# One feature tile at a time in the first stage of a diffusion backbone: token rows loaded first, root chains moved, context tiles moved into the second half

## The chip, the cores and the metric

The kernel runs on one core of a Trainium2 chip. The metric is the device time of one execution in microseconds; lower is better. A core has five engines with a queue each: TensorE (PE in the profile; its weight loads are PEld), VectorE (DVE), ScalarE (ACT), GpSimd (POOL) and SyncE (SP, which here only starts transfers). They run side by side and wait for each other through semaphores. Data lies in SBUF (128 partitions); matmuls write to PSUM banks of 128 x 512 numbers, which ScalarE and VectorE read out.

## The reference, cut to what matters

```python
silu_c, silu_cc = silu(c), silu(c_ctx)
# layer 0, attention; layer 1 (a convolution branch on the latent tokens only) is not touched
shift, scale, gate = split((silu_c @ ada_w[0] + ada_b[0])[:, None, :], 3)
h_lat = rmsnorm(x, norm_g[0]) * (1 + scale) + shift            # x: 1024 tokens x 1024
shift_c, scale_c, _ = split(silu_cc @ ada_w[0] + ada_b[0], 3)
h_ctx = rmsnorm(ctx, norm_g[0]) * (1 + scale_c) + shift_c      # ctx: 256 tokens x 1024
proj = h_lat @ w_in                                            # q (16 heads), k, v (4 heads each), z
kv_c = h_ctx @ w_in[:, q_end:v_end]
o = windowed_attention(rope(q), rope(k), v, kc, vc, sink)      # window 128, all context keys, a sink
x = x + gate * ((o * silu(z)) @ w_out)
```

Everything is float32. A product of two float32 matrices is made of three matmuls in the rounded type fp32r: high part by high part, high by low and low by high, where the low part is what rounding left over.

## The kernel before

**Order of the work.** The kernel is one straight program: a first stage that normalises and modulates the tokens and computes the first heads' projections, then attention over 16 heads with the remaining projections filled in between, the output projection, the convolution branch and its projection. The change touches the first stage alone, and a few lines that reach into the second. The first stage works on features in tiles of 128 (`KT` = 8 of them, index `kt`) and on tokens in halves of 512.

**Who sets the order.** The kernel is scheduled by a framework, which orders each engine's instructions by a model of time, except for the engines that `pin(...)` names: `InOrder` then keeps these in the order of the program. TensorE is always pinned; `pin("PVA")` (line 477) adds VectorE and ScalarE for the beginning of the stage, `pin("PV")` (line 497) leaves ScalarE to the scheduler for the rest of it. Since all engine calls go through `InOrder.call`, every row of the profile has line 89; rows are told apart by their tiles.

**Names in the rows.** `x_page` are token rows (128 tokens x 1024, float32), `araw_page` modulation weights, `arow_half` the row of modulation sums, `mod` the shift and scale columns of a tile, `wraw_page`, `whi_page`, `wlo_page` a projection weight and its high and low part, `hf_page`, `hh_page`, `hl_page` a modulated feature tile (full, high, low), `hch_page`, `hcl_page` the same for context, `junk_page` the squares, whose sums are kept. PSUM tiles are `psg` (two banks), `pso` (`ps_o(0)` and `ps_o(1)`, one bank each) and `pss` (two tiles of two banks). `zerr_page` are zeros on which `spin(n)` runs n matmuls that compute nothing used.

**The stage, step by step.**
- Loads (lines 317 to 334) are started on SP: `ada_load(pr)` fetches the shift and scale weights of a pair of feature tiles (8 transfers of 256 KB in runs of 1 KB, and the biases), `load_rows` token rows (512 KB each), `wsA.load` a projection weight (512 KB in runs of 512 bytes). The first pair's modulation weights stand ahead of the first half's token rows.
- `sums` squares rows on ScalarE, `rstd_of` makes 1/sqrt of the mean by a root on ScalarE and six small operations on VectorE, `scale_rows` multiplies the rows by it.
- `ada_mm(pr)` multiplies silu(c) by the modulation weights of a pair (8 matmuls of 512 columns in four column groups), VectorE adds the biases, `ada_cols(pr)` turns the row into columns with a small matmul each, VectorE writes them to `mod`.
- `turn` transposes four token blocks of a feature tile, `x_tile` modulates the result: ScalarE writes the high part, VectorE the full tile, VectorE or GpSimd the low part. ScalarE and VectorE read the same PSUM bank one after the other.
- `x_mm(kt, half, acc, which)` multiplies feature tile `kt` with the weights of k, q and v (9 matmuls of 512 columns).
- The loop over pairs `pr` (line 500) does this for the first half of the tokens, with everything for pair `pr + 1` issued ahead. At `pr == 2` the roots of the second half's rows (`normalise(xs1, ...)`) stand on VectorE behind the add of pair 3 and ahead of its modulation columns. The context's tiles (`c_tile`) are made in the last two pairs.
- Then `finished0` takes k, q and v out of PSUM (the rotary step `rope` copies halves of a head between partitions by DMA), `ctx0("k", 0)` projects the context's keys, and the second loop does `x_mm` for the other 512 tokens, with `ctx0("v", 2)` at `kt == 3`. It ends with `scores(0, 0)`, the first scores of attention.

## Time and profile before

| | us |
|---|---|
| median of three runs | 1727.83 (1724.6, 1727.83, 1729.25) |
| the profiled execution | 1728.0 |
| its span | 1726.2 |
| TensorE's granted clock over the span | 0.993 |
| VectorE, ScalarE, GpSimd busy | 1090.0, 873.8, 899.1 |
| moved by DMA | 242.44 MB |

How to read it: the page gives one execution. Busy time of a matmul is from its issue to its modelled end, so a matmul of 512 columns has some 0.39 us though the next one starts 0.23 after it. Rows in order of time have the start, the duration of the whole group, the engine, the operation with written <- read tiles, the shape, the count, and in brackets how long the engine stood idle and for whom. Rows of stretches give the busy time of each engine with the number of instructions, then TensorE's granted clock, the share of time in which the DMA engines were busy, and GB/s.

### The profile page before, as it was taken

What the parts mean: (1) busy time and instruction counts of PE and PEld (TensorE: products, weight loads), DVE (VectorE), ACT (ScalarE), POOL (GpSimd) and SP (SyncE); (2) the same over time, 40 slices, a digit from 0 to 9 for tenths busy, and PEclk for the clock granted to TensorE, in tenths of its full rate; (3) what the DMA queues carried; (4) which work ended last, traced back from release to release, by engine and by line L of the source; (5) the groups of instructions that cost most, each with busy time, mean ns of one, the idle gap of its engine ahead of it and who ended that gap; (6) DMA issues with size and microseconds to landing.
All of it is one profiled execution on the core that took longest, in us unless ns stands there. A gap on an engine that the chain in (4) does not pass through costs nothing.

```text
span 1726.2 us, 23896 instructions
## 1 busy us (share of the span) xinstructions
PE 1692.5 (98%) x8420; PEld 1423.5 (82%) x8420; DVE 1090.0 (63%) x2077; ACT 873.8 (51%) x1532; POOL 899.1 (52%) x745
## 2 busy tenths in 40 slices
PE   8899999999999999999999999999999999999997
PEld 5688888888888888888888888888888888787886
DVE  4555553555355453555315179999999999867823
ACT  4555544555355444545334355565665564466731
POOL 1255654666546564643101257999898888130400
PEclk9999999999999999999999999999999999999999
DMA  9233442444334443436776733011121302377971
GB/s 335 85 110 123 155 140 76 136 151 148 96 124 141 156 129 93 141 115 210 261 252 247 247 94 107 21 50 37 43 80 37 92 31 80 122 260 244 330 269 49
DMA packets 195323, 242.44 MB, mean 140 GB/s; under 512 B 11798, under 2 KB 126790, under 8 KB 195204
## 3 DMA queue, kind: packets, MB, share of 16 engines
q1 hardware_dynamic: 188516, 230.10, 40.1%
q10 hardware_dynamic: 6688, 10.83, 2.5%
q8 instruction: 66, 1.08, 0.3%
q14 instruction: 53, 0.43, 0.1%
HBM read 188.70 MB, written 41.69 MB: 133 GB/s over the span
## 4 chain that ended last, share of the span: by engine, by line
PE 91%; DMA 3%; ACT 2%; DVE 2%; POOL 1%; issue 1%; SPq 0%; ACTq 0%; DVEq 0%; POOLq 0%
PE psg L89 47%; PE pss L89 24%; PE pso L89 20%; DMA low_page<-in_conv_w_out_dram 1%; DMA rope_half<-rope_half 1%; POOL rope_half L89 0%; DMA wo_page<-in_conv_w_out_dram 0%; DMA x_page<-in_x_dram 0%; DMA araw_page<-in_ada_w_dram 0%; SPq L89 0%; ACT junk_page L89 0%; ACT hh_page L89 0%; ACT lhi_half L89 0%; ACT x_page L89 0%; POOL wlo_page L89 0%
## 5 line engine op out<-in xcount | busy, mean ns | idle before, releaser
L89 POOL TENSOR_TENSOR odd_half<-odd_half,prod_half 128x513 f32<-128x513 f32 (+2 forms) x252 | 314.2, 1255 | 23.0 <-ACT prod_half L89 9.6
L89 PE MATMUL psg<-hh_page,whi_page 128*128 128x512 f32 x600 | 236.2, 394 | 0.0
L89 PE MATMUL psg<-hl_page,whi_page 128*128 128x512 f32 x600 | 235.1, 392 | 0.0
L89 PE MATMUL psg<-hh_page,wlo_page 128*128 128x512 f32 x600 | 234.6, 391 | 0.0
L89 ACT ACTIVATE prod_half<-ubuf,dww 128x513 f32<-128x513 f32 (+2 forms) x252 | 165.7, 675 | 115.9 <-POOL odd_half L89 112.1
L89 POOL TENSOR_TENSOR wlo_page<-wraw_page,whi_page 128x512 fp32r<-128x512 f32 (+1 forms) x106 | 177.5, 1691 | 88.2 <-ACT whi_page L89 60.3
L89 POOL TENSOR_SCALAR p_page<-p_page,sc 128x640 f32<-128x640 f32 (+1 forms) x128 | 99.6, 778 | 225.6 <-DVE sc L89 218.4
L89 PE MATMUL psg<-h2h_page,whi_page 128*128 128x512 f32 x464 | 181.9, 392 | 0.0
L89 PE MATMUL psg<-h2h_page,wlo_page 128*128 128x512 f32 x464 | 180.6, 389 | 0.0
L89 PE MATMUL psg<-h2l_page,whi_page 128*128 128x512 f32 x464 | 180.6, 389 | 0.0
L89 DVE SCALAR_TENSOR_TENSOR pss<-ubuf,dww,pss 128x512 f32<-128x512 f32 (+3 forms) x270 | 172.6, 672 | 0.1
L89 DVE SCALAR_TENSOR_TENSOR pss<-ubuf,wsum,pss 128x512 f32<-128x512 f32 (+3 forms) x270 | 172.0, 672 | 0.2
L89 DVE TENSOR_TENSOR ptlo<-pss,pthi 128x640 fp32r<-128x640 f32 (+1 forms) x144 | 103.5, 719 | 86.3 <-ACT pthi L89 85.1
L89 ACT ACTIVATE p_page<-p_page,sc 128x641 f32<-128x641 f32 (+1 forms) x128 | 102.6, 802 | 76.9 <-DVE sc L89 72.6
L89 ACT ACTIVATE pthi<-pss 128x640 fp32r<-128x640 f32 (+1 forms) x144 | 88.8, 617 | 103.7 <-PE pss L89 97.3
L89 PEld LDWEIGHTS psg<-hh_page,wlo_page 128*128 128x128 f32 x600 | 113.1, 188 | 24.7
L89 PEld LDWEIGHTS psg<-hh_page,whi_page 128*128 128x128 f32 x600 | 113.1, 188 | 19.5
L89 PEld LDWEIGHTS psg<-hl_page,whi_page 128*128 128x128 f32 x600 | 113.2, 189 | 18.7
L89 ACT ACTIVATE whi_page<-wraw_page 128x1024 fp32r<-128x1024 f32 x88 | 92.5, 1052 | 58.5 <-PE psg L89 20.9
L89 PE MATMUL pso<-h2h_page,whi_page 128*128 128x512 f32 x304 | 118.3, 389 | 0.0
L89 PE MATMUL pso<-h2l_page,whi_page 128*128 128x512 f32 x304 | 118.3, 389 | 0.0
L89 PE MATMUL pso<-h2h_page,wlo_page 128*128 128x512 f32 x304 | 118.3, 389 | 0.0
(239 smaller groups left out, 4008.6 us busy)
## 6 DMA issues: line engine op xcount, KB each, us to landing
wraw_page<-in_conv_w_in_dram SPq DMA_DIRECT2D x48, 512.0 KB
wraw_page<-in_attn_w_in_dram SPq DMA_DIRECT2D x40, 512.0 KB
wol_page<-wolA SPq DMA_DIRECT2D x32, 512.0 KB
wo_page<-in_attn_w_out_dram SPq DMA_DIRECT2D x32, 512.0 KB
wo_page<-in_conv_w_out_dram SPq DMA_DIRECT2D x32, 512.0 KB
wol_page<-wolC SPq DMA_DIRECT2D x32, 512.0 KB
rope_half<-rope_half ACTq DMA_DIRECT2D x80, 128.0 KB
araw_page<-in_ada_w_dram SPq DMA_DIRECT2D x32, 256.0 KB
```

Source lines behind the costliest of these rows:

```text
L89: r = f(*a, **k)
```

## The change

- **Single feature tiles.** `ada_load`, `ada_mm`, `ada_cols` and `mods` work on one feature tile instead of a pair: 4 transfers of 256 KB, now in runs of 512 bytes; 8 matmuls of 256 columns; an add of 256 columns; two column matmuls. The loop runs over `kt`, with the modulation of `kt + 1` issued around the matmuls of `kt`. All the low parts of the first half's tiles are made by VectorE (before, every second one by GpSimd).
- **Loads.** Token rows go first, then the modulation weights of tile 0, then projection weights and further tiles; then the small vectors (biases and such, before in the middle of the loop), the second half's rows and the context's. The mask and the sinks are loaded by SP instead of ScalarE's queue.
- **Scaling of rows.** The first half's four rows are scaled by VectorE, GpSimd, ScalarE, GpSimd (before V, V, A, A), ahead of `ada_mm(0)`; the spins are redistributed.
- **Roots.** The squares of the second half's rows are issued at `kt == 4`, their roots and scaling at the end of `kt == 6`, behind the tile work of feature 7 on VectorE and ahead of the second half's first tile.
- **Context.** Its rows are squared at `kt == 6`, scaled at the second half's `kt == 0`, its tiles made at `kt` 2 to 5 of the second half's loop, two in each, and `ctx0("k")` and `ctx0("v")` follow at 6 and 7.
- **Second half.** `finished0` takes v out first; the rotary steps start one tile later; the pages of q and v are allocated at `kt == 5`, and the weight of the next projection is loaded there (before at 0) and split at 6 (before at 5).

```diff
-    def ada_load(pr):
-        R[pr] = hp.alloc(F32, None, "arow")
-        G.memset(R[pr][:, 0:512], 0.0)
-        araw[pr] = [pg.alloc(F32, [2, 2, 256], "araw") for _ in range(4)]
-        for i in range(4):
+    def ada_load(kt):
+        if kt % 2 == 0:
+            R[kt // 2] = r = hp.alloc(F32, None, "arow")
+            G.memset(r[:, 0:512], 0.0)
             for j in range(2):
...
+        araw[kt] = [pg.alloc(F32, [4, 2, P], "araw") for _ in range(2)]
+        for i in range(2):
+            for j in range(2):
+                SY.dma_start(out=araw[kt][i][:, :, j],
+                             in_=ada_w[0, i * 512:i * 512 + 512, j * D + kt * P:j * D + kt * P + P]
                              .rearrange("(k p) n -> p k n", p=P))
...
     spin(4)
+    xs0 = load_rows(x[0, 0:512], 4)
     ada_load(0)
-    xs0 = load_rows(x[0, 0:512], 4)
     wsA.load()
     ada_load(1)
     wsA.load()
     wsA.load()
     ada_load(2)
+    ada_load(3)
+    ada_load(4)
+    ada_load(5)
...
-    ada_load(3)
+    ada_load(6)
+    ada_load(7)
+    vec_pg = load_vecs()
+    xs1 = load_rows(x[0, 512:1024], 4)
     cx = load_rows(ctx[0], 2)
...
+    def ada_mm(kt):
+        o = ps_o(0)[:, 0:256]
+        for i in range(2):
+            rv = araw[kt][i].rearrange("p a b c -> p a (b c)")
+            for k in range(4):
+                PE.matmul(o[32 * k:32 * k + 32], c32[:, 4 * i + k, :], rv[:, k], start=i == 0, stop=i == 1,
+                          tile_position=(0, 32 * k))
...
+        r = R[kt // 2][:, kt % 2 * 256:kt % 2 * 256 + 256]
         tt(V, r, o, r, ALU.add)
...
     pin("PVA")
-    ada_split(0)
-    spin(10)
+    spin(28)
     ss0 = sums(xs0, (A, A, A, A))
+    r0 = rstd_of(ss0, D, 4)
+    scale_rows(xs0, r0, (V, G, A, G))
     ada_mm(0)
     ada_cols(0)
-    spin(18)
-    r0 = rstd_of(ss0, D, 4)
-    wsA.split(lambda: scale_rows(xs0, r0, (V, V, A, A)))
-    xs1 = load_rows(x[0, 512:1024], 4)
     tps = [turn(xs0, kt, ps_g) for kt in range(2)]
-    for kt in range(2):
-        x_tile(tps[kt], kt, 0, V)
-    spin(5)
-    pg.free(zer_r)
-    x_mm(0, 0, acc0, (0,))
-    x_mm(1, 0, acc0, (0,))
+    x_tile(tps[0], 0, 0, V)
+    wsA.split()
+    spin(4)
+    ada_mm(1)
+    x_mm(0, 0, acc0, (0,))
+    ada_cols(1)
+    x_tile(tps[1], 1, 0, V)
     pin("PV")
-    ada_split(1)
+    spin(6)
+    pg.free(zer_r)
     wsA.split()
     wsA.split()
-    for pr in range(NPR):
...
-        if pr == 2:
-            normalise(xs1, ss1, (G, G, A, G))
...
+    ctodo = deque(range(KT))
+    for kt in range(1, KT):
+        nx = kt + 1
+        if nx < KT:
+            ada_mm(nx)
+        x_mm(kt, 0, acc0, (0,))
+        if kt == 1:
+            x_mm(0, 0, acc0, (1,))
+        if nx < KT:
+            tp = turn(xs0, nx, ps_g)
+            ada_cols(nx)
+            x_tile(tp, nx, 0, V)
+        else:
+            turn_vecs()
+            x_tile(turn(xs1, 0, ps_g), 0, 1, V)
+        x_mm(kt, 0, acc0, (1,))
+        if kt == 1:
+            x_mm(0, 0, acc0, (2,))
+        x_mm(kt, 0, acc0, (2,))
+        if kt == 4:
             ss1 = sums(xs1, (A, A, A, A))
-        if pr == 2:
+        if kt == 6:
             pg.free(*xs0)
             cos, sin = (pg.alloc(F32, [1024], n) for n in ("cos", "sin"))
...
+            normalise(xs1, ss1, (G, V, A, V))
+            ssc = sums(cx, (A, A))
+    x_tile(turn(xs1, 1, ps_g), 1, 1, V)
...
-    A.dma_start(out=mask[:, 0:640], in_=k_mask)
-    A.dma_start(out=sink, in_=attn_sink.partition_broadcast(P).rearrange("p o h -> p (o h)"))
+    SY.dma_start(out=mask[:, 0:640], in_=k_mask)
+    SY.dma_start(out=sink, in_=attn_sink.partition_broadcast(P).rearrange("p o h -> p (o h)"))
...
-    finished0(0, acc0, ropes=ropes0)
-    ctx0("k", 0)
+    finished0(0, acc0, (2, 0, 1), ropes0)
...
     for kt in range(KT):
         x_mm(kt, 1, acc1, range(3))
         if kt + 2 < KT:
             x_tile(turn(xs1, kt + 2, lambda: ps_o(kt % 2)), kt + 2, 1, G if kt % 2 and kt > 1 else V)
-        if kt > 2 and ropes0:
+        if kt == 0:
+            normalise(cx, ssc, (V, A))
+        if kt > 3 and ropes0:
             ropes0.popleft()()
-        if kt == 3:
-            ctx0("v", 2)
-        if kt >= 2 and tails:
+        if 1 < kt < 6:
+            c_tile(ctodo.popleft(), ps_s)
+            c_tile(ctodo.popleft(), lambda: ps_o((kt + 1) % 2))
+        if kt == 5:
+            for i in (1, 2):
+                d0[i].extend(target("kqv"[i], 0))
+            pg.free(*xs1)
+            wsA.load()
+        if kt >= 6 and tails:
             tails.pop(0)()
-        if kt == 0:
-            wsA.load()
-        if kt == 5:
-            pg.free(*xs1)
+        if kt == 6:
             wsA.split()
+            ctx0("k", 0)
+        if kt == 7:
+            ctx0("v", 2, lambda: ps_o(1))
         if kt == KT - 1:
             scores(0, 0)
```

137 lines of the change are left out of this document (44 added, 93 removed).

## The prediction

> **What bounds the kernel now.** I read the page first (busy shares, then the chain that ended last), then the busy time by stage, then the order of time of the stages that the change touches.
>
> ```profile
> span 1726.2 us, 23896 instructions
> PE 1692.5 (98%) x8420; PEld 1423.5 (82%) x8420; DVE 1090.0 (63%) x2077; ACT 873.8 (51%) x1532; POOL 899.1 (52%) x745
> PE 91%; DMA 3%; ACT 2%; DVE 2%; POOL 1%; issue 1%; SPq 0%; ACTq 0%; DVEq 0%; POOLq 0%
> ```
>
> TensorE is busy 98% of the span and carries 91% of the chain of waits, so outside the first stage only its own work counts. The profiled execution took 1728.0 us, 1.8 us more than its span; the three runs have their median at 1727.83, so sums against 1728.0 need no correction.
>
> The table of stretches cuts the span at marks of the first stage: first real matmul (24.82), third feature tile (35.62), fifth (43.59), seventh (57.23), second half (67.87), first scores (94.23).
>
> ```profile
> core 0: us, PE busy (x) PEld busy (x) DVE busy (x) ACT busy (x) POOL busy (x), PEclk, DMA share, GB/s
> 0.00:24.82 24.82, 18.06 (x69) 10.90 (x70) 8.18 (x22) 12.42 (x18) 3.55 (x11) 0.96 0.88 298
> 24.82:35.62 10.80, 10.80 (x68) 6.28 (x66) 7.36 (x12) 3.68 (x4) 0.04 (x1) 0.94 1.10 375
> 35.62:43.59 7.97, 7.97 (x55) 5.51 (x51) 3.42 (x7) 3.52 (x6) 1.26 (x1) 1.00 1.04 401
> 43.59:57.23 13.64, 9.50 (x46) 7.64 (x43) 6.72 (x20) 9.31 (x20) 5.73 (x5) 0.75 0.43 152
> 57.23:67.87 10.64, 9.76 (x64) 8.22 (x62) 7.62 (x16) 7.76 (x17) 1.38 (x2) 1.00 0.37 96
> 67.87:94.23 26.36, 23.53 (x128) 19.12 (x126) 15.57 (x22) 10.15 (x18) 5.78 (x4) 1.00 0.21 60
> 94.23:200.00 105.77, 105.77 (x588) 91.96 (x587) 59.60 (x138) 57.61 (x123) 64.37 (x59) 1.00 0.41 127
> ```
>
> From 94.23 on TensorE is never idle, at full clock, with 0.41 of the DMA engines busy. So what the change wins or loses before the first scores is carried to the end one for one, and nothing behind it is to be won. The question is when the first scores start. Two features matter 7.97 us (3.98 each) in the undisturbed stretch 35.62 to 43.59, 13.64 in the next: that is the stall.
>
> ```profile
> 47.75 0.42 PE L89 MATMUL pso<-ident,x_page 128*128 128x128 f32 x2
> 49.95 0.17 DVE L89 TENSOR_SCALAR ms<-ssx 128x4 f32<-128x4 f32 x1 [3.17 <-ACT junk_page L89]
> 51.84 0.66 PE L89 MATMUL pso<-ident,x_page 128*128 128x128 f32 x2 [3.67 <-DVE mod L89]
> 49.00:50.00 1.00, 0.00 (x0) 0.00 (x0) 0.05 (x1) 1.00 (x3) 0.00 (x0) 0.96 1.10 393
> 50.00:51.00 1.00, 0.00 (x0) 0.00 (x0) 0.63 (x4) 0.36 (x2) 0.00 (x0) 0.50 0.89 356
> 55.00:56.00 1.00, 1.00 (x4) 0.75 (x3) 1.00 (x3) 0.00 (x0) 0.00 (x0) 0.50 0.00 0
> 56.00:57.00 1.00, 1.00 (x7) 0.86 (x6) 0.04 (x1) 0.00 (x0) 0.00 (x0) 0.63 0.00 0
> ```
>
> TensorE waits 3.67 us because the modulation of features 6 and 7 stands on VectorE behind the roots of the second token half, and those wait for ScalarE's squares of the rows (VectorE stood 3.17 us for them). The granted clock falls to one half within two microseconds of the last matmul and stays there until about 56.4, so the matmuls after the stall cost double: some 2 us more. The stall with its echo is 13.64 - 7.97 = 5.7 us.
>
> **The change, part by part.** I follow the new program in three terms: when the third feature tile starts, from there to the second half, and the second half.
>
> *Term 1, the prologue.* Token rows now go first on SP's queue, ahead of 2.1 MB of modulation weights.
>
> ```profile
> 2.86 4.02 SPq L89 DMA_DIRECT2D araw_page<-in_ada_w_dram  x8
> 17.33 1.06 ACT L89 ACTIVATE junk_page<-x_page 128x1024 f32<-128x1024 f32 x1
> 18.51 0.17 DVE L89 TENSOR_SCALAR ms<-ssx 128x4 f32<-128x4 f32 x1 [2.74 <-ACT junk_page L89]
> 19.77 0.16 DVE L89 TENSOR_TENSOR r<-rr,rq 128x4 f32<-128x4 f32 x1
> 51.52 3.31 POOL L89 TENSOR_SCALAR x_page<-x_page,r 128x1024 f32<-128x1024 f32 x3 [4.16 <-issue]
> DMA packets 984, 1.00 MB, mean 335 GB/s; under 512 B 60, under 2 KB 965, under 8 KB 984
> DMA packets 1936, 1.05 MB, mean 351 GB/s; under 512 B 35, under 2 KB 1936, under 8 KB 1936
> DMA packets 349, 1.26 MB, mean 421 GB/s; under 512 B 41, under 2 KB 41, under 8 KB 349
> 28.43 1.23 DVE L89 TENSOR_TENSOR wlo_page<-wraw_page,whi_page 128x1024 fp32r<-128x1024 f32 x1 [0.32 <-ACT whi_page L89]
> ```
>
> The three packet rows are the DMA view of 8 to 11, 23 to 26 and 41 to 44 us: mostly 1 KB packets of modulation weights at 335 GB/s in the filling pipe, mostly 512-byte packets of projection weights at 351, 4 KB token rows at 421. The fourth token row is squared at 17.33 now, when it lands; without the 2.1 MB before it (6.8 us at 310 GB/s, a mean of the slow beginning) it lands at about 10.5. Square and roots take 17.33 to 19.93, 2.6 us: the scales are there at 13.1. Two of the four rows are now scaled by GpSimd, one after the other, at 1.10 each: 15.4. Transposes (0.3) and ScalarE's first half tile bring VectorE to its first tile at 16.7. From there VectorE's hand-written order is the path until the third feature tile is ready. Its pieces stand in the rows below: a tile costs 0.81 + 0.69, a low part of a weight 1.23, the modulation columns 0.6 on TensorE with the wait, 0.38 on VectorE, then ScalarE's 0.78. The add of 256 columns has no row; it lies between nothing and the 0.69 of 512 columns, I take 0.45. Written out: 1.5 + 1.23 + 0.45 + 0.6 + 0.38 + 0.8 + 1.5 + 2.46 + 0.45 + 0.6 + 0.38 + 0.8 + 1.5 = 12.7. That gives 29.4, and 1.1 for TensorE's pieces at half clock in so broken a stretch: **30.5 instead of 35.62, 5.1 us won** (bounds 29.4 and 33, the latter if the half clock also doubles the nine matmuls ahead of it). The modulation weights of three features and the three projection weights (4.7 MB) must be there by then: behind the rows, at 351 GB/s, they land at about 23.5, hidden by 2 us of VectorE's work.
>
> *Term 2, six tiles to the second half.* The same work is issued one feature at a time: adds, copies and matrix pieces are halved in width and doubled in number. TensorE's work per feature stays 3.98 us. But what used to have two features' cover now has one:
>
> ```profile
> 30.96 0.95 PE L89 MATMUL pso<-vt,arow_half 128*128 128x2 f32 x8
> 31.95 0.16 DVE L89 COPY mod<-pso 128x4 f32<-128x4 f32 x1 [1.69 <-PE pso L89]
> 32.33 0.78 ACT L89 ACTIVATE hh_page<-psg,mod 128x512 fp32r<-128x512 f32 x1 [3.93 <-DVE mod L89]
> 33.14 0.81 DVE L89 TENSOR_SCALAR hf_page<-psg,mod 128x512 f32<-128x512 f32 x1 [0.78 <-ACT hh_page L89]
> 33.99 0.69 DVE L89 TENSOR_TENSOR hl_page<-hf_page,hh_page 128x512 fp32r<-128x512 f32 x1
> 33.77 1.92 PE L89 MATMUL pso<-araw_page,c_page 128*32 128x512 f32 x16
> 35.62 0.50 PE L89 MATMUL pss<-hh_page,whi_page 128*128 128x512 f32 x1
> ```
>
> From the end of the columns (31.91) to the low tile (34.68) pass 2.77 us, 2.6 with one scale operation fewer. The loop closes over two matmuls on that tile (0.46), a transpose (0.4) and the next columns (0.5 to 0.6): 4.0 to 4.1 us, against 3.98 of TensorE work. I take 4.1, five times 20.5, so the low tile of feature 7 is ready at **51.0** (bounds 20 and 24: the latter if ScalarE's four squares of 1.05 us, placed in this loop, each hold up a half tile by 0.9). The weights do not pace it: 1.05 MB per feature at 351 GB/s is 3.0 us; if that cover went, the loop would run at the DMA's pace.
>
> Then the roots. They now follow the last tile on VectorE instead of standing before it. The wait for the squares is gone (they were issued two features earlier), but the roots themselves (1.42 from 18.51 to 19.93) and two rows scaled by VectorE (1.5) are in front of the transposes of the second half's first tile, which stand on TensorE ahead of 6 of the 9 last matmuls. TensorE reaches them 0.85 after the low tile, the rows are ready at 2.95: a new stall of 2.1 us. What is behind it: the six matmuls, the next transposes, and the evacuation of the value projection that frees the bank for the second half. With transposes (0.35), six matmuls at half clock (2.6), transposes and the wait for that evacuation (0.9) it is **6.8 us to the second half, at 57.8** (5.6 at full clock, up to 8).
>
> The clock drop is taken from the 49 to 50 us row, where less than 2 us of idling were enough. The Trainium skill, "TensorE: Matmul & The Clock Gate", section "Why this matters for your kernels", says that only gaps above some 3 us throw the array back to half clock. Going by that page the second half would start 1.2 us earlier and the total would be 1719.3; the row disagrees with it, and I go by the row.
>
> Before, the second half began at 67.87. Of the 10.1 us between, 2.9 are the context keys' projection (24 matmuls at 0.12, rows below), which now runs inside the second half.
>
> *Term 3, the second half.* TensorE's work: 2.5 for each of 8 features less two transposes (19.3), four transposes for context tiles in four features (1.5), 48 matmuls on context at 0.12 (5.8) and 0.4 for values: 26.9.
>
> ```profile
> 80.13 0.28 PE L89 MATMUL psg<-hcl_page,whi_page 128*128 128x256 f32 x1
> 80.25 0.28 PE L89 MATMUL psg<-hch_page,wlo_page 128*128 128x256 f32 x1
> L89 ACT ACTIVATE hf_page<-pso,mod 128x256 f32<-128x256 f32 x8 | 4.2, 561 | 0.0
> L89 ACT ACTIVATE hch_page<-hf_page 128x256 fp32r<-128x256 f32 x8 | 3.1, 418 | 0.0
> L89 DVE TENSOR_TENSOR hcl_page<-hf_page,hch_page 128x256 fp32r<-128x256 f32 x8 | 3.9, 520 | 0.6 <-ACT hch_page L89 0.6
> ```
>
> ScalarE gets per feature 0.78 + 2 x (0.56 + 0.42) = 2.74 in four features of 2.9 us: just covered. What is not covered is the beginning, where the evacuations for the rotary step, four copies issued on ScalarE's queue and the context's roots come between the half tiles; I take 2.0 us of stalls. The stretch of before idled 26.36 - 23.53 = 2.8 us; bounds 0.5 and 6. **28.9 us, first scores at 86.7.**
>
> *Costed at nothing:* the table of small vectors, the mask and the sinks now go through SP's queue, at most 10 short issues behind the features' loads; they are needed after 50 us, and all loads together (15.3 MB from about 4 us on, between 335 and 421 GB/s) are over by 41 to 50. If that were not so, the sinks' negation would hold VectorE, and the second half's tiles behind it. The load of the next weights moves from feature 0 to feature 5; its 0.5 MB have 10 us until used.
>
> **Sum:** 94.23 - 86.7 = 7.5 us, from 1728.0: 1720.5.
>
> **The rivals.**
> (a) *No clock drop, no stalls.* 29.5 + 20 + 5.6 + 27.5 = 82.6, so 1716.4. For it: all transfers are ahead, the loop is nearly even. Against: the stretch 43.59 to 57.23.
> (b) *ScalarE paces the second half*, or the squares stand ahead of the half tiles. If the context tile is done in full before the next half tile, a feature costs 2.74 and about 1.3 of waits and transposes, 4.0 instead of 2.9; four features give 4.5 us back: 1725.0. For it: 2.74 of 2.9. Against: half tiles are issued with priority.
> (c) *The change moves the stall but does not shorten it:* term 2 at its bounds (24, 8) gives back 4.7, 1725.2.
> (d) *Slower: the feature loads pace the loop.* Its place is the DMA engines between 13 and 50 us. Runs of 512 bytes instead of 1 KB double the packets; the first scores follow the last feature's landing by 4.2 + 6.8 + 28.9 = 39.9 us. 10 MB behind 10.0 us: at 225 GB/s nothing is won, below that it is slower; at 180 GB/s it lands at 65.5, 1739. For it: the feature loads ran at 335 or less until 11 us. Against: 351 GB/s in the row with just such packets.
>
> **How the numbers follow.** A measurement here can tell 0.3%, 5.2 us, from no change. Forecast 48%, (a) 20%, (b) 12%, (c) 10%, (d) 10%. The forecast alone spreads over 1717.5 to 1724, five sixths of it faster than 1722.8; with (a): 0.61 faster. The rest of the forecast with (b) and (c) nearly whole: 0.30. (d): 0.09. The range of 8 in 10 runs from 1714 to 1728: (a) with a bit more, (b), (c), and nothing of (d).
>
> **What would show it.** Right: third feature tile at about 30.5; a period of 4.1 us in the loop with short waits of TensorE for the low tile; one wait of about 2 us for scaled rows near 52, with the half clock behind; the second half from 58; first scores near 87; the same work behind it. Wrong: waits of TensorE on modulation weights after 25 us (d); ScalarE without idle time between 60 and 75 (b); TensorE waiting on squares (c); or, at first scores near 87, a total that did not move, so that the stages behind took it back.

## The result, and the profile after

The changed kernel took 1728.09 us in the median of 14 runs against 1727.26 for the kernel before on the same chip: ratio 1.0008, interval 0.9998 to 1.0018. A second series gave 1.0013 (1.0005 to 1.0022). That is no gain, and within 0.3% no loss; predicted was 1720.5, range 1714 to 1728. The profiled execution took 1727.67 us.

The head of the page after (busy time of TensorE, then the chain of waits by engine):

```profile
span 1725.9 us, 24046 instructions
...
PE 1694.5 (98%) x8489; PEld 1425.7 (83%) x8489; DVE 1096.1 (64%) x2090; ACT 873.3 (51%) x1531; POOL 895.4 (52%) x741
...
PE 91%; DMA 3%; DVE 2%; SPq 2%; ACT 1%; issue 1%; POOL 1%; ACTq 0%; DVEq 0%; POOLq 0%
```

TensorE bounds the kernel as before. Its table of stretches starts at the second feature tile and is cut at the marks that answer to those of before (third feature tile, fifth, end of TensorE's longest wait, seventh, second half, first scores; columns as before):

```profile
25.12:30.95 5.83, 5.82 (x43) 4.02 (x39) 3.84 (x7) 0.78 (x1) 0.00 (x0) 1.00 1.11 329
30.95:39.46 8.51, 8.51 (x71) 5.75 (x67) 4.01 (x10) 1.56 (x2) 0.00 (x0) 1.00 0.92 267
39.46:47.44 7.98, 4.38 (x38) 2.86 (x34) 0.96 (x5) 1.81 (x3) 0.00 (x0) 0.97 0.70 218
47.44:55.17 7.73, 6.96 (x33) 4.79 (x33) 3.60 (x7) 6.15 (x11) 0.00 (x0) 0.59 0.87 346
55.17:66.91 11.74, 8.41 (x41) 5.91 (x37) 7.28 (x18) 4.20 (x8) 1.61 (x1) 0.88 0.25 96
66.91:97.52 30.61, 28.80 (x165) 24.12 (x166) 22.88 (x37) 17.66 (x37) 5.38 (x4) 0.99 0.31 84
97.52:200.00 102.48, 101.44 (x565) 87.99 (x564) 58.46 (x135) 55.22 (x117) 61.94 (x57) 1.00 0.38 118
```

The third tile starts at 30.95 (before 35.62; predicted 30.5), and two features then take 8.51. So far the gain of 4.7 us is there. The next two take 7.98 + 7.73 = 15.71 us with TensorE idle for 3.60 of the first 7.98 and a clock of 0.59 in the rest. The second half begins at 66.91 (before 67.87, predicted 57.8), the first scores at 97.52 (before 94.45 by the same row; the prediction's mark of 94.23 stands one matmul earlier). The change is 3.1 us behind there, and yet the total is level. Two questions follow: where did the 10.8 us between 86.7 and 97.52 go, and why does the total not show the 3.1?

TensorE's waits after, in order of time (start, duration, tiles, and in brackets the idle time ahead and for whom):

```profile
47.44 0.80 PE L89 MATMUL pss<-hh_page,whi_page 128*128 128x512 f32 x1 [3.60 <-ACT hh_page L89]
...
59.74 0.49 PE L89 MATMUL pss<-hl_page,whi_page 128*128 128x512 f32 x1 [1.07 <-DVE hl_page L89]
...
62.84 0.88 PE L89 MATMUL psg<-ident,x_page 128*128 128x128 f32 x4 [2.11 <-POOL x_page L89]
...
73.89 0.50 PE L89 MATMUL pss<-hl_page,whi_page 128*128 128x512 f32 x1 [1.07 <-DVE hl_page L89]
...
77.08 0.72 PE L89 MATMUL pss<-ident,x_page 128*128 128x128 f32 x2 [0.62 <-DVE x_page L89]
```

ScalarE's timeline at the first of them:

```profile
45.57 1.06 ACT L89 ACTIVATE junk_page<-x_page 128x1024 f32<-128x1024 f32 x1 [7.36 <-DMA x_page<-in_x_dram]
...
46.63 0.76 ACT L89 ACTIVATE hh_page<-psg,mod 128x512 fp32r<-128x512 f32 x1
```

SP's issues in the changed kernel (start, duration of the group, tiles, count):

```profile
32.70 5.35 SPq L89 DMA_DIRECT2D araw_page<-in_ada_w_dram  x8
...
42.37 1.99 SPq L89 DMA_DIRECT2D x_page<-in_x_dram  x4
```

ScalarE does the half tile of feature 5 (`hh_page`, 46.63) only after the first square of the second half's rows (`junk_page`, 45.57), for which it stood 7.36 us: the row had not landed. The columns of feature 5 (`mod`) were written by 41.7, 5 us earlier. SP issued the rows at 42.37, behind all modulation weights and six small vectors.

### The profile page after: what moved, and what is told of

Read it like the earlier page. It is cut to its first block, busy times and chain, and to the rows that moved or that the text cites. A ratio compares the mean times of both kernels' runs of the same rounds, so it can differ in the third digit from the quotient of the medians.

```text
span 1725.9 us, 24046 instructions
## 1 busy us (share of the span) xinstructions
PE 1694.5 (98%) x8489; PEld 1425.7 (83%) x8489; DVE 1096.1 (64%) x2090; ACT 873.3 (51%) x1531; POOL 895.4 (52%) x741
## 4 chain that ended last, share of the span: by engine, by line
PE 91%; DMA 3%; DVE 2%; SPq 2%; ACT 1%; issue 1%; POOL 1%; ACTq 0%; DVEq 0%; POOLq 0%
PE psg L89 47%; PE pss L89 23%; PE pso L89 20%; SPq L89 2%; DMA low_page<-in_conv_w_out_dram 1%; DMA rope_half<-rope_half 1%; DMA x_page<-in_x_dram 0%; DMA araw_page<-in_ada_w_dram 0%; POOL rope_half L89 0%; DVE hf_page L89 0%; DMA ozf_page<-ozd 0%; DMA wraw_page<-in_attn_w_in_dram 0%; ACT lhi_half L89 0%; DVE hl_page L89 0%; DVE ptlo L89 0%
```

## The experiments

The first scores and a later row tell the stage: `qh_page<-rope_half` in the attention behind it stands at 125.04 before; "shift" is this row's distance from that. The ratio is to the kernel before on the same chip.

| kernel | first scores | shift at 125 | ratio (95%) |
|---|---|---|---|
| before, first and again | 94.45, 94.44 | 0.0, 0.0 | 1, 1.0002 (0.9993 to 1.0012) |
| changed | 97.52 | +4.7 | 1.0008 (0.9998 to 1.0018) |
| changed again | 100.25 | +7.3 | 1.0013 (1.0005 to 1.0022) |
| changed, vectors last | 96.28 | +3.3 | 1.0012 (1.0000 to 1.0024) |
| changed, rows ahead | 96.14 | +3.3 | 1.0002 (0.9990 to 1.0013) |
| changed, squares late | 94.53 | +1.5 | 1.0000 (0.9991 to 1.0009) |
| changed, 1 KB runs | 95.71 | +2.9 | 1.0004 (0.9993 to 1.0014) |
| changed, spin in the gap | 96.75 | +6.8 | 1.0020 (1.0011 to 1.0029) |
| changed, rows ahead, roots earlier | 93.41 | +0.5 | 0.9975 (0.9966 to 0.9985) |
| all remedies, 1 KB runs | 91.26 | -1.7 | 0.9983 (0.9973 to 0.9993) |
| mixed loads | 92.79 | -0.1 | 0.9972 (0.9961 to 0.9983) |
| 512-byte loads, squares by hand | 91.83 | -1.1 | 0.9970 (0.9958 to 0.9982) |
| the same, context squares later | 90.51 | -2.3 | 0.9965 (0.9953 to 0.9977) |
| before, token rows first | 95.36 | +1.8 | 1.0012 (1.0003 to 1.0022) |
| before, roots behind | 96.05 | +2.6 | 1.0018 (1.0010 to 1.0027) |
| before, 30 matmuls more | 101.03 | +6.6 | 1.0022 (1.0013 to 1.0032) |

First scores and shift are from one profiled execution each; the two of the changed kernel differ by 2.7 us, those of before by nothing.

Between these two marks the changed kernel loses another 1.6 us (from +3.1 to +4.7), and every version made from it loses about 1.5 to 1.7 there (the one with the spin 4.5). What stands between them is not the same work as before: transposes of the context's values, which stood ahead of the first scores in the kernel before (at 83.52), now stand behind them, and TensorE waits for their evacuation:

```profile
99.58 0.44 PE L89 MATMUL pso<-ident,vf_half 128*128 128x128 f32 x2 [1.04 <-ACT vf_half L89]
```

From the first scores to the later row TensorE has 31.20 us busy and 1.04 idle in the changed kernel, 30.59 and none before. So the first scores flatter the change by 1.6 us, and the shift at 125 is the fairer mark.

### What made the rows late: their place, or the transfers

```diff
-    vec_pg = load_vecs()
     xs1 = load_rows(x[0, 512:1024], 4)
     cx = load_rows(ctx[0], 2)
+    vec_pg = load_vecs()
```

> The changed kernel, with the six short loads of the small vectors issued behind the second half's token rows and the context rows. Theory: what undid the gain is ScalarE's first square of these rows, which stood in front of feature 5's half tile until 45.57, because SP issued the rows only at 42.37. Here they are issued at about 38.1, the first square starts at about 41.5, TensorE's 3.60 us wait for that half tile shrinks below 0.7, its half-clock echo goes, the loop keeps its 4.25 us period, the second half starts at about 59.5 (66.9 in the changed kernel) and the first scores come at about 90 (97.5); the total is about 1720.5. Rival 1, the transfers: the DMA engines were 0.83 to 0.99 busy until 40, so rows issued earlier land no earlier than 44; the wait stays above 2 us and the first scores at 95 to 97. Rival 2, given back behind: the first scores come at 90, but the total stays within 1726 to 1729, since waits in the attention take their place.

```diff
+    xs1 = load_rows(x[0, 512:1024], 4)
     ada_load(6)
     ada_load(7)
-    vec_pg = load_vecs()
-    xs1 = load_rows(x[0, 512:1024], 4)
     cx = load_rows(ctx[0], 2)
+    vec_pg = load_vecs()
```

> The changed kernel, with the second half's token rows issued ahead of the modulation weights of features 6 and 7 (and the small vectors behind the context rows). Theory: the rows are issued at about 32.7 and squared when they are wanted, no half tile waits for a row; the second half starts at about 59.5, the first scores come at about 90, the total is about 1720.5. Rival 1, the transfers: what is put ahead only moves the lateness; the weights of features 6 and 7 come 3 us later and TensorE waits 2 to 3 us for them near 44 to 48, first scores at 93 to 96. Rival 2, given back behind: first scores at 90, total within 1726 to 1729.

With the vectors last, SP issued the rows at 39.64, 2.7 us earlier, and ScalarE still waited for them until 46.07: the transfers, not SP's place, set the landing in this execution (rival 1). In the run with longer transfers further down, rows issued at 39.56 were squared from 43.00 on. The weights of the early features had come later in this execution (waits of 0.86 and 2.21 us near 24 to 27), so feature 5 waited only 0.54, but the first scores gained 1.2 us where 7.5 were expected.

With the rows ahead of features 6 and 7, SP's issue was at 32.29, and ScalarE's timeline and TensorE's read:

```profile
38.88 1.06 ACT L89 ACTIVATE junk_page<-x_page 128x1024 f32<-128x1024 f32 x1 [3.83 <-DMA x_page<-in_x_dram]
...
41.17 0.76 ACT L89 ACTIVATE hh_page<-psg,mod 128x512 fp32r<-128x512 f32 x1
```
```profile
41.98 0.50 PE L89 MATMUL pss<-hh_page,whi_page 128*128 128x512 f32 x1 [1.30 <-ACT hh_page L89]
...
43.55 0.50 PE L89 MATMUL pss<-hl_page,whi_page 128*128 128x512 f32 x1 [1.07 <-DVE hl_page L89]
...
61.03 0.95 PE L89 MATMUL psg<-ident,x_page 128*128 128x128 f32 x4 [2.10 <-POOL x_page L89]
```

The scheduler moved two squares along with the rows, in front of feature 4 now, and the same stall came back one feature earlier, at 1.30 us. It is not as cheap as it looks: behind it and the 1.07 us for the low tile the granted clock was down to one half from 44.6 to 48:

```profile
45.00:46.00 1.00, 1.00 (x4) 0.90 (x5) 0.29 (x2) 0.22 (x1) 0.00 (x0) 0.50 0.98 290
```

The roots' stall of 2.10 is untouched. In neither run did the first scores come at the 90 expected. Here they came at 96.14, which was the time of rival 1, though TensorE did not wait for the weights of features 6 and 7.

The bandwidth is in the stretches from 10 to 40 us (last column GB/s). The kernel before:

```profile
10.00:20.00 10.00, 8.14 (x38) 4.54 (x34) 2.15 (x11) 5.78 (x10) 0.00 (x0) 1.00 1.04 376
20.00:30.00 10.00, 8.50 (x39) 5.26 (x40) 8.22 (x10) 5.80 (x6) 0.00 (x0) 0.83 1.11 373
30.00:40.00 10.00, 10.00 (x66) 7.34 (x66) 4.10 (x11) 1.92 (x3) 1.30 (x1) 1.00 1.07 381
```

The changed kernel:

```profile
10.00:20.00 10.00, 8.12 (x57) 4.78 (x55) 5.10 (x13) 4.86 (x9) 2.68 (x2) 0.83 1.14 342
20.00:30.00 10.00, 8.98 (x64) 6.04 (x59) 5.99 (x12) 3.26 (x4) 0.00 (x0) 1.00 1.13 336
30.00:40.00 10.00, 10.00 (x85) 6.46 (x85) 5.18 (x12) 1.56 (x2) 0.00 (x0) 1.00 0.95 279
```

Before moved 3.76 + 3.73 + 3.81 = 11.3 MB, the changed kernel 3.42 + 3.36 + 2.79 = 9.6 MB, while its DMA engines were busy for about as large a share (0.95 to 1.14 against 1.04 to 1.11). 1.7 MB are 4.6 us at 376 GB/s. Run length is not the only difference, since the stretches of before also hold token rows in 4 KB packets. The Trainium skill, "DMA: Bandwidth & Descriptors", section "Specifications", puts the least transfer for full rate at 512 bytes. The runs of just that size moved less here than the mix of before. Hence the next run: pairs of features loaded in runs of 1 KB, used one by one.

```diff
-        araw[kt] = [pg.alloc(F32, [4, 2, P], "araw") for _ in range(2)]
+        araw[kt // 2] = [pg.alloc(F32, [2, 2, 256], "araw") for _ in range(4)]
...
-                             in_=ada_w[0, i * 512:i * 512 + 512, j * D + kt * P:j * D + kt * P + P]
+                             in_=ada_w[0, i * 256:i * 256 + 256, j * D + kt * P:j * D + kt * P + 256]
```

> The changed kernel with the modulation weights loaded by pairs of features, in the 1 KB runs of the kernel before, while tiles are still worked one by one; ScalarE's order is that of the changed kernel, its one square in front of feature 5's half tile included. Theory (run length): what made the second half's rows late is that 512-byte runs load at 279 to 342 GB/s between 10 and 40 us where 1 KB runs loaded at 373 to 381. Here the rate is above 360, the rows are issued by about 37 and the first square starts by about 41.5; TensorE's wait for feature 5 (3.60 us) falls below 1, the second half starts at about 60 (66.9), the first scores come at about 90.5 (97.5), the total is about 1721. Rival (issue time): SP needs 0.6 to 0.8 us for each issue because there are many of them, whatever the runs; rows issued no earlier than 41, wait above 2.5, first scores above 96.

Its stretches, and ScalarE's first square of the second half's rows:

```profile
10.00:20.00 10.00, 7.18 (x37) 4.23 (x36) 2.25 (x9) 3.66 (x6) 2.69 (x2) 0.89 1.02 330
20.00:30.00 10.00, 10.00 (x62) 6.42 (x61) 6.06 (x11) 4.39 (x5) 0.00 (x0) 0.77 1.07 365
30.00:40.00 10.00, 9.47 (x71) 6.20 (x69) 5.71 (x13) 1.56 (x2) 0.00 (x0) 1.00 0.94 307
```
```profile
43.00 1.06 ACT L89 ACTIVATE junk_page<-x_page 128x1024 f32<-128x1024 f32 x1 [0.34 <-DMA x_page<-in_x_dram]
```

10.0 MB, an average of 334 GB/s and not the 360 expected; the first row was squared at 43.00, and no wait of feature 5 above 0.3 us was left. But pairs come in as one, and feature 2 was ready 4 us later (ScalarE's half tile at 32.7 instead of 28.3). First scores 95.71. With the changed kernel's own order of loads five profiles moved 8.8 to 9.6 MB in these 30 us, so the 10.0 of this one profile point to a cost of the short runs. It is the smaller part: 0.45 of the 1.7 MB came back, and what set the rest the runs do not show. What longer runs gave they took back at the start.

### The square in front of the half tile

Loads as changed; ScalarE is kept in the order of the program, with the rows' squares behind the half tiles of features 6 and 7. The context's squares now stand right behind them, ahead of the roots (in the program of the changed kernel they stand behind the roots):

```diff
+    pin("PVA")
     for kt in range(1, KT):
...
             x_tile(tp, nx, 0, V)
+            squares({5: (0, 1), 6: (2, 3)}.get(kt, ()))
+            if kt == 6:
+                ssc = sums(cx, (A, A))
...
-        if kt == 4:
-            ss1 = sums(xs1, (A, A, A, A))
...
-            ssc = sums(cx, (A, A))
```

> The changed kernel with ScalarE's four squares of the second half's rows placed by hand behind the half tiles of features 6 and 7 (two each), loads as they were. Theory (square in front): no half tile waits for a row, TensorE does not wait for feature 5, and the low tile of feature 7 is ready at about 52 (59.6 in the changed kernel); the roots then wait for the last squares and the stall in front of the second half's first tile grows from 2.1 to 4 to 5 us; second half at about 62.5, first scores at about 93, total about 1724. Rival (all loads late): the stall appears at the weights of features 6 and 7 as well, first scores at 96 or later.

TensorE's waits there, and VectorE's in the roots:

```profile
53.75 0.50 PE L89 MATMUL pss<-hl_page,whi_page 128*128 128x512 f32 x1 [1.08 <-DVE hl_page L89]
...
59.21 1.11 PE L89 MATMUL psg<-ident,x_page 128*128 128x128 f32 x4 [4.47 <-POOL x_page L89]
```
```profile
56.41 0.18 DVE L89 RECIPROCAL rr<-sq 128x4 f32<-128x4 f32 x1 [2.00 <-ACT sq L89]
```

No half tile waited. The low tile of feature 7 was taken at 53.75, against 59.74 and 62.41 in the two profiles of the changed kernel, 6.0 and 8.7 us earlier. Counted from the third tile, so that early waits for weights drop out, it came 21.9 us behind it, against 28.8 and 29.6: 6.9 and 7.7 us are what that one square cost. Of it the roots took back 2.4, a wait of 4.47 instead of 2.11. The size was expected, the reason only in part: the rows' squares were over at 54.2, and 2.0 us more went by while ScalarE did the context's two squares ahead of the root. First scores 94.53 (expected 93); total level with before.

### The roots, and the clock behind a gap

Eight matmuls without use fill the roots' gap:

```diff
+            held = ps_g()
+            for _ in range(8):
+                PE.matmul(held, wsA.hl[0][0][:, 0], Hh[0][:, 0:512], start=True, stop=True)
-            x_tile(turn(xs1, 0, ps_g), 0, 1, V)
+            x_tile(turn(xs1, 0, lambda: held), 0, 1, V)
```

> The changed kernel with eight matmuls of 128x512 without use put in TensorE's wait for the scaled rows, ahead of the first transposes of the second half (they write the bank that the transposes overwrite). Theory (half clock behind the gap): eight at 0.23 us fill 1.8 of the 2.11 us, the granted clock stays at 1.00, the six matmuls behind go at 0.23 instead of 0.43 us, and the second half starts 1.5 us sooner behind the low tile of feature 7: 5.7 us after it instead of 7.2. Rival (the clock falls for another reason than the gap): the clock is 0.50 behind the gap all the same, and the second half starts no sooner.

The granted clock (third number from the right) in the changed kernel behind the gap that ends at 62.84:

```profile
63.00:64.00 1.00, 1.00 (x6) 0.70 (x6) 0.69 (x4) 0.25 (x1) 0.00 (x0) 1.00 0.00 0
64.00:65.00 1.00, 1.00 (x4) 0.78 (x3) 0.44 (x1) 0.82 (x2) 0.00 (x0) 0.53 0.00 0
66.00:67.00 1.00, 0.84 (x5) 0.44 (x3) 0.10 (x1) 0.74 (x2) 0.00 (x0) 0.50 0.41 94
```

With the spin, TensorE's row in the gap and then the stretches behind it:

```profile
61.65 2.11 PE L89 MATMUL psg<-hh_page,whi_page 128*128 128x512 f32 x8
```
```profile
64.00:65.00 1.00, 1.00 (x6) 0.70 (x6) 0.70 (x4) 0.24 (x1) 0.00 (x0) 1.00 0.00 0
66.00:67.00 1.00, 0.75 (x6) 0.50 (x4) 0.96 (x2) 0.71 (x2) 0.00 (x0) 1.00 0.00 0
```

Without the gap the clock stays at 1.00, and the second half starts 66.80 - 60.73 = 6.07 us behind the low tile of feature 7 instead of 7.17. So 1.1 us of the roots' cost is clock, and filling the gap takes the drop away. The total did not follow (1.0020). Directly behind the first scores this execution had one wait more:

```profile
98.07 0.38 PE L89 MATMUL pss<-kvc_page,qh_page 128*128 128x256 f32 x1 [0.80 <-DVE kvc_page L89]
...
100.21 0.69 PE L89 MATMUL pso<-ident,vf_half 128*128 128x128 f32 x2 [1.03 <-ACT vf_half L89]
```
```profile
101.00:102.00 1.00, 1.00 (x4) 0.71 (x4) 0.42 (x2) 0.82 (x1) 1.00 (x2) 0.50 0.76 154
```

Behind these two the clock was at 0.50 from 100.0 to 103.4, and at 125 the execution was 6.8 late. In the changed kernel, with the second wait alone, it stayed at 1.00. So two waits of about 1 us close together were followed by the same half clock as one of 2.1.

Moving the roots away altogether:

```diff
+        if kt == 5:
+            normalise(xs1, ss1, (G, G, A, G))
...
-            normalise(xs1, ss1, (G, V, A, V))
```

> The kernel before this one (token rows ahead of features 6 and 7), and the second half's roots and scalings moved from behind the last tile to behind feature 6's tile on VectorE, with three rows scaled by GpSimd and one by ScalarE. Theory: the roots' own stall (2.11 us in the changed kernel, with 1.6 us of half clock behind it) goes as well: second half at about 56, first scores at about 86.7, total about 1717. Rival 1: the roots come so early that they wait for squares again, and VectorE holds feature 7's tile behind them by 1 to 3 us: first scores at 88 to 91. Rival 2, given back behind: total within 1726 to 1729 whatever the first scores.

Rows ahead as above, the squares still stand in front of feature 4 (wait 1.63), again with half clock behind it (44.7 to 48), and VectorE holds feature 7 by 0.76 and 1.31; but the 2.1 us gap and its echo are gone, and the total is 0.25% below before, the first that is. First scores 93.41, not the 86.7 expected.

### Parts of the change alone, on the kernel before

```diff
-    ada_load(0)
     xs0 = load_rows(x[0, 0:512], 4)
+    ada_load(0)
```

> The kernel before the change, with only the first half's token rows issued ahead of the first modulation weights. Theory (the rows alone carry the first term): the third feature tile starts 3 to 5 us earlier than 35.62; but the rows of the second half are issued no earlier than before (36.87) and are squared until about 49.8 as before, so the roots stall VectorE and TensorE longer by about as much, and the second half starts near 67, first scores near 93.5, total about 1727. Rival: the whole of the gain comes through, third tile at 31, first scores at 89 to 90, total about 1723.

The expectation fell: the third half tile came at 38.7 instead of 32.3, since the first pair of weights (2.1 MB) now lay behind the rows. Rows first paid here only together with narrow first tiles. The stage made up most of it (shift +1.8): the second half's rows came when they had come before (squared from 40.1 on, before 40.3), so the roots held TensorE for 0.93 us only instead of 3.67.

```diff
-        if pr == 2:
-            normalise(xs1, ss1, (G, G, A, G))
...
         if pr == 2:
+            normalise(xs1, ss1, (G, G, A, G))
             pg.free(*xs0)
```

> The kernel before the change, with only the second half's roots and scalings moved behind VectorE's tile work of features 6 and 7. Theory (a stall moved, shortened): TensorE's 3.67 us wait at 51.84 goes, a wait of 2 to 4 us for the scaled rows comes in front of the second half's first tile; second half at about 64 (67.9), first scores at about 90.5 (94.2), total about 1723.5. Rival: the half tile of feature 6 still stands behind the squares on ScalarE until 49.8, and the new stall costs as much as the old one: first scores within 1.5 us of 94.2, total 1726 to 1729.

The wait of 3.67 went and one of 4.04, with two more of 0.62 and 0.41, came in front of the second half's first tile, whose rows GpSimd scaled one after another. The roots behind the tile work alone move the stall and make it larger: 1.0018, the rival's side.

### How much of a delay reaches the end

> The changed kernel once more, to see how much the first scores vary from one execution to the next (97.5 in the first profile). Theory (order sets it): the first square of the second half's rows stands in front of feature 5's half tile again and TensorE waits over 2.5 us for it; first scores within 1.5 us of 97.5, total 1728 as before. Rival (a chance of that execution): no such wait, first scores below 94.

> The kernel before the change once more, for the same reason (first scores at 94.4 in its first profile, and a wait of 3.17 us near 577 and of 0.4 near 760 behind them). Theory (the stages behind differ by more than chance): the wait near 577 is above 2.6 us again (2.0 and 1.5 in the profiles of the changed kernel and of one made from it), the first scores come within 1.5 us of 94.4. Rival: that wait is at 2 us or less here too, so that the stages behind are alike.

The square stood in front again, with 4.39 us of wait, though the first scores came 2.7 us later than in the first profile and not within the 1.5 expected. The changed kernel's stage is 4.7 to 7.3 us behind at the row of 125 us, its total 0.8 to 2.7. To separate, the kernel before with a pure delay:

```diff
+            held = ps_g()
+            for _ in range(30):
+                PE.matmul(held, wsA.hl[0][0][:, 0], Hh[0][:, 0:512], start=True, stop=True)
-            x_tile(turn(xs1, 0, ps_g), 0, 1, V)
+            x_tile(turn(xs1, 0, lambda: held), 0, 1, V)
```

> The kernel before the change with thirty matmuls of 128x512 without use ahead of the second half's first tile: a delay of 30 x 0.23 = 6.9 us and nothing else; 0.6 of it fall into a wait that is there. First scores at about 100.7 (94.4). Theory (one for one, the prediction's assumption): the total rises by 6.3 us, to a ratio of 1.0036. Rival (given back behind): the waits behind, 9.7 us in the profile of before, shrink since their transfers come no later than now, and the total rises by 4 us or less, to a ratio below 1.0023.

A delay of 6.6 us at the row of 125 raised the total by 0.22%, 3.8 us (interval 2.2 to 5.5): not one for one. Most of what is taken back shows at one wait near 577: ScalarE waits there for output weights of the convolution branch, and behind these on its queue stands the work on TensorE's next operand. Before, ScalarE, TensorE and a stretch behind:

```profile
574.79 1.15 ACT L89 ACTIVATE lhi_half<-low_page 128x512 fp32r<-128x512 f32 x2 [5.91 <-DMA low_page<-in_conv_w_out_dram]
```
```profile
577.44 0.45 PE L89 MATMUL pss<-kh_page,qh_page 128*128 128x384 f32 x1 [3.17 <-DVE ptlo L89]
```
```profile
579.00:580.00 1.00, 1.00 (x4) 0.80 (x3) 1.00 (x3) 0.55 (x2) 1.00 (x2) 0.50 0.85 239
```

The same three of the changed kernel:

```profile
578.15 1.15 ACT L89 ACTIVATE lhi_half<-low_page 128x512 fp32r<-128x512 f32 x2 [4.72 <-DMA low_page<-in_conv_w_out_dram]
```
```profile
580.80 0.44 PE L89 MATMUL pss<-kh_page,qh_page 128*128 128x384 f32 x1 [1.98 <-DVE ptlo L89]
```
```profile
583.00:584.00 1.00, 1.00 (x6) 0.84 (x5) 1.00 (x2) 0.60 (x2) 1.00 (x2) 1.00 0.21 71
```

TensorE in the kernel before with the delay:

```profile
583.37 0.45 PE L89 MATMUL pss<-kh_page,qh_page 128*128 128x384 f32 x1 [1.81 <-DVE ptlo L89]
```

The wait is 3.17 us and throws the clock to 0.50 for some 3 us; the shorter ones, 1.98 and 1.81, leave it at 1.00. A wait shorter by 1.2 us with no echo behind it gives back 3 us: the changed kernel's shift goes from +4.8 at 525 to +1.7 at 611, and in the kernel with the delay it goes from +7.3 at 570 to +4.4 at 584. In three profiles of kernels before without delay (again, rows first, roots behind) the wait was 2.86, 4.81 and 2.79, in the profiles of the kernels made from the changed one 1.45 to 2.39. Why it is shorter there, though the instructions around it stand in the same order, the runs do not settle.

### Versions that beat both

> All remedies together on the changed kernel: modulation weights in 1 KB runs, the second half's rows ahead of the weights of features 6 and 7, two squares behind each of the half tiles of features 4 and 5, the roots behind feature 6's tile, small vectors last. Theory: the first stage loses neither to the rows nor to the roots: third tile at 30.5 to 31, low tile of feature 7 at about 52.5, second half at about 56, first scores at about 86.5, total about 1716.5. Rival (given back behind): first scores at 86.5, but total above 1720, since the stages behind take up what was won; the kernel with the first scores at 93.4 ran 1722.5.

> A version meant to beat both: the one with all remedies, but features 0 and 1 loaded singly as in the changed kernel (with pairs from the start the third tile began about 1.5 us late), the others by pairs in 1 KB runs, and the second half's roots placed on VectorE between the add and the columns of feature 7, with ScalarE's scaled row behind feature 7's half tile. Theory: third tile near 31, waits of 0.77 and 1.33 us at feature 7 shrink to 0.4 and less, second half at about 58, first scores at about 88.5 (91.3 in the version with all remedies), total about 1720. Rival (given back behind): first scores near 88.5 and total no lower than 1722.5, the best so far.

> The changed kernel's own loads (single features, 512-byte runs), with the second half's rows ahead of features 6 and 7, two squares each placed by hand behind the half tiles of features 4 and 5, and the roots between the add and the columns of feature 7. Theory: third tile near 31 as in the changed kernel, no half tile behind a row, low tile of feature 7 near 53, second half at about 57.5, first scores at about 88, total about 1719 (ratio 0.995). Rival (given back behind): first scores at 88 and the total no lower than 1722.5.

The first has all remedies: 91.26, not 86.5, since pairs delay the start as seen (waits of 0.7 to 0.8 for weights near 15 and 28) and the roots hold feature 7 by 0.77 and 1.33. Mixed loads: the second pair came later still, four waits of 0.7 to 1.2 near 25 to 29. With the changed kernel's loads the third tile was early (ScalarE at 28.6), and then the context's squares stood in front of feature 7, on ScalarE and then on TensorE, with 1.33 us for the low tile and half clock (58.5 to 61.9) behind it:

```profile
50.67 1.06 ACT L89 ACTIVATE junk_page<-x_page 128x1024 f32<-128x1024 f32 x1 [1.92 <-DMA x_page<-in_ctx_dram]
```
```profile
55.29 0.49 PE L89 MATMUL pss<-hh_page,whi_page 128*128 128x512 f32 x1 [1.92 <-ACT hh_page L89]
```

```diff
             x_tile(tp, nx, 0, V)
-            if kt == 5:
-                ssc = sums(cx, (A, A))
...
             scale_rows(xs1[2:3], r1[:, 2:3], (A,))
+            ssc = sums(cx, (A, A))
```

> The version with hand-placed squares and the changed kernel's own loads (first scores 91.8, total 0.9970 of before), with the two squares of the context rows moved from behind feature 6's half tile to behind feature 7's and the last scaled row: in that version they waited for rows that landed at 50.67 and held feature 7's half tile, and TensorE 1.92 us. Theory (a square in front of a half tile, a second time): that wait goes, no half clock behind it, second half at about 58.5 (62.0), first scores at about 88.5 to 89.5, total about 1719 (ratio 0.9955). Rival: the weights of feature 7, which landed late too (waits of 0.57 and 0.84), hold feature 7 as long; first scores above 90.5, ratio 0.997.

TensorE from feature 7 to the second half:

```profile
56.76 0.50 PE L89 MATMUL pss<-hl_page,whi_page 128*128 128x512 f32 x1 [1.30 <-DMA sin_page<-in_k_sin_dram]
...
60.40 0.50 PE L89 MATMUL pss<-hh_page,whi_page 128*128 128x512 f32 x1 [0.25 <-ACT vf_half L89]
```

That wait went: the clock stays at 1.00 and the second half starts at 60.40, although in this execution a weight was 3.03 us late near 25. 1719.47 us, ratio 0.9965: about 6 us below before (4 to 8). It is the lowest ratio, but within the intervals of the two versions ahead of it (0.9970 and 0.9972).

## Why the prediction was wrong, step by step

**Third tile at 30.5: right** (30.95). Rows squared by 11.5, scales at 13.07 (predicted 13.1), GpSimd's first row 1.59 beside VectorE's and its second 1.11 (predicted 1.10 each), the add 0.42 (0.45), weights late by 1.0 (predicted: hidden by 2 us). The weights are the loose part, and that the number came so close is in part luck: with the same order of loads the third tile came at 32.83 in the second profile and at 34.49 with the vectors last.

**Low tile of feature 7 at 51.0: wrong, 59.74. This is the step that failed** (28.8 us from the third tile, outside the bounds of 20 and 24), in the sentence "The wait for the squares is gone (they were issued two features earlier)". Issued earlier in the program is not earlier in time: the squares' rows were loaded last. Their loads were costed at nothing because all loads "are over by 41 to 50"; in ScalarE's order the rows were needed from 41.7 on, so that very interval held the loss. Of the 8.7 us, 0.45 is the third tile, 5 x (4.26 - 4.1) = 0.8 the period, and some 7.0 the square with its half clock (15.71 us for two features, less 8.51, is 7.2). Late squares removed it. The bound in which each square holds up a half tile by 0.9 priced a square that runs, not one that waits. The rate of 351 GB/s was taken from one window of 512-byte packets; between 10 and 40 us it was 279 to 342, so a mild form of rival (d) was at work, though the loop itself was not paced by it.

**Roots, 6.8 us: right in mechanism, 7.17.** The stall was 2.11 (predicted 2.1), half clock behind it. That the 2.1 came out is in part luck: it ended with GpSimd's row, which took 1.61 us instead of 1.1 beside VectorE's, and VectorE's two rows took 2.28 instead of 1.5. With the clock held it is 6.07 (predicted 5.6 for full clock).

The half clock after a gap, which the prediction took from a row, held (its row of 56 to 57, at 0.63, puts the end of that half clock at 56.7 rather than 56.4). The Trainium skill, "TensorE: Matmul & The Clock Gate", section "Why this matters for your kernels", warns of gaps above some 3 us, which put the array back to half clock. The traces differ: 2.10 and 2.11 were enough here, and so were 0.80 and 1.03 close together.

**Second half 28.9: too short, 30.61.** TensorE's own work was near the 26.9 (a feature took 2.5, the 48 context matmuls 0.12 each), but the stalls were sized 2.0 and cost 3 to 3.5: 1.8 show as idle (1.07 for a low tile, 0.62 for scaled context rows), and the rest counts as busy, in restarts (a matmul right behind a wait has 0.50 instead of 0.39) and the end of the half clock. Rival (b), ScalarE as the pace, did not come: TensorE is not idle from 78.5 to the first scores.

**One for one: wrong.** "Nothing behind it is to be won" rested on an idle-free stretch up to 200. Behind it TensorE idled 9.7 us in the profile of before (from 100 to 1700), and some of these waits shrink. This is why the 4.7 and 7.3 us lost by 125 became 0.8 and 2.7 at the end. Nor is it "the same work behind it": 1.6 us of context work moved behind the first scores. The last sentence of what would make the prediction wrong named a total that stages behind hold; it held in the other direction.

**Rivals.** No rival priced the outcome: (b) and (c) stop at 1725.0 and 1725.2, and (d) reaches 1728 only at 225 GB/s, where this profile has 279 or more. In cause it is the second half of (b) (squares ahead of half tiles) and the sign of (c) (TensorE waiting on squares), with the wait added that neither priced. The best version (1719.5, about 6 us below before) shows that most of the predicted 7.5 us was there to be had, from a schedule that the change did not have.

## What to carry to other kernels

When an operation moves on an in-order queue, ask what it reads and when that lands, and then what stands behind it: a short square for a late row in front of a half tile cost about 7 us. Fix the place by hand where a scheduler's model of transfers is off, and put work that waits for late data behind the work that feeds the bounding engine. Before carrying a gain to the end one for one, look at all waits behind, and test it with a pure delay.

## What was not expected of the hardware

One wait just above 2 us can already halve the clock. At the same wait near 577, in 17 profiles, the seven gaps of 1.45 to 1.98 us left the granted clock at 1.00; of six between 2.00 and 2.39, four (2.00, 2.00, 2.30, 2.33) were followed by 0.50 for about 3 us and two (2.20, 2.39) were not; all four from 2.79 on were. The roots' gaps of 2.10 and 2.11 were followed by it in each of the five profiles that had them.

The length of a single gap does not tell all of it. Shorter waits that followed each other closely were followed by 0.50 too: 1.30 and 1.07 (rows ahead), 1.63 and 1.07 (rows ahead, roots earlier), 1.92 and 1.33 (squares by hand), 0.80 and 1.03 (spin in the gap), each for about 3.4 us; 0.54 and 1.08 (vectors last, 47.94 and 49.51) were not. The five gaps of the roots had a wait of 1.07 or 1.08 about 1 us ahead of them as well. No run here tests where the line lies.

VectorE and GpSimd held each other up when they scaled rows at the same time. Behind the roots of the changed kernel VectorE took 0.75 us for its first row and 1.61 for its second, GpSimd 1.61 for its one; before, with the other engine not scaling, two rows took VectorE 1.42 and one took GpSimd 1.12.
